# Gate and up products of a decoder layer's last two row groups: VectorE's order written out, both pairs in one chain of blocks, whole weight sums per transfer, input sums stored unsplit

## The chip, the cores and the metric

The kernel runs on one core of a Trainium2 chip. The metric is the device time of one execution in microseconds. Beside it stands one profiled execution, in which the start, the length and the waits of every instruction were recorded. The engines are TensorE (PE, its weight loads are PEld), VectorE (DVE), ScalarE (ACT), GpSimd (POOL) and SyncE (SP), whose instruction queue issues nearly all transfers of the part of the program that is changed.

## The reference

One layer of a hybrid decoder on 2048 rows of 1024 numbers in float32. The change is in the feed-forward part:

```python
h = h + _rmsnorm(y, g_post_mix[l])
f_in = _rmsnorm(h, g_pre_ffn[l])
gt = jnp.einsum("bsd,df->bsf", f_in, w_gate[l])
up = jnp.einsum("bsd,df->bsf", f_in, w_up[l])
f = jnp.einsum("bsf,fd->bsd", jax.nn.silu(gt) * up, w_down[l])
h = h + _rmsnorm(f, g_post_ffn[l])
```

`w_gate` and `w_up` are 1024 x 2816, `w_down` is 2816 x 1024.

## The kernel before, in words

**The arithmetic.** Every float32 operand of a product is split into a high part H (a copy to a narrower type, on ScalarE) and a low part L (the difference, on GpSimd or VectorE). A product is three products of halves, L x H, H x H and H x L. Here that is 4 slices of the inner dimension x 3 = 12 matmuls of 128x128 by 128x512.

**The fast multiplication.** The rows are taken in four groups of 512. Groups 0 and 1 form the first pair, groups 2 and 3 the second. For a pair, each block of the weights (two column tiles of 128, `i` = 0 for gate and 1 for up, `j` = 0 to 10) is a 2x2 matrix product, done by a Strassen-Winograd scheme with seven products (numbered 1 to 7) instead of eight. Weight sums S (numbers 3, 5, 6, 7) and `w_down` sums were computed and stored to DRAM during the attention part. Product 1 plus 2 (called `c11`) and, for the first pair, product 4 (`p4`) were computed there too and are only loaded.

**The stage that is changed** is the tail after attention. `five(g, B, todo)` (L1078) runs over 22 blocks of a pair: four products per block for the first pair (6, 5, 7, 3), five for the second (6, 5, 7, 4, 3). It is called twice, for g = 0 and then for g = 2, and each call begins with a first block of its own and ends by storing what is left.

**One block.** Two PSUM banks are used, `b2` and `b3`. Product 6 goes into `b2`, product 5 into `b3`. VectorE keeps `u2 = b2 + s1` (L1103; `s1` is one half of c11). Product 7 is added into `b2`; then VectorE reads `u3 = b2 + s1` (L1116), for the first pair adds `u3` to `p4` (L1119), and forms `u3 = b3 + u3` (L1120). Product 6 of the next block comes before product 4 (added into `b2`, so after L1116) and product 3 (added into `b3`, so after L1120). L1131 and L1134 read the final `b2` and `b3`. The four results of a gate block are put through a sigmoid on ScalarE (L1052) and multiplied on VectorE (L1053); those of an up block are multiplied into them (L1057). After each up block `hidden` forms the hidden sums with four VectorE additions, all between SBUF tiles (L1063 to L1066), and queues seven tiles for storing.

**Weights.** `weights` (L1019) loads a block's four sums S as four transfers into two `raw` tiles of 128x1024, copies each to `wH` (L1044, ScalarE) and subtracts to `wL` (L1045, GpSimd). There are three `wH` and three `wL` buffers and two are used per block, so a split can begin when an older product ends: the first of a block's two when product 3 of two blocks before ends, the second when product 5 of the block before ends.

**Beside the first pair** run the rest of the mixing part of group 3 (`residual`, L702, VectorE's L712 among it) and, for k = 0 to 3, `input_sums` (L860): it transposes rows of groups 2 and 3 on TensorE (L865), forms five input sums on VectorE and GpSimd (L887 to L897), splits each into H and L, and stores both. They are loaded again as operands of the second pair.

**What sets the order.** The tile framework orders each engine's queue by a simulated time of readiness. The matmuls of `product` are pinned by `keep_in_program_order`: each behind the instruction that stands before it on its engine as the code is written. VectorE, ScalarE, GpSimd and SyncE are ordered by the framework. `flush(2)` after each product puts up to two stores into SP's queue.

## Time and profile before

| | us |
|---|---|
| median of 3 runs | 2673.92 |
| lowest and highest run | 2673.45, 2678.8 |
| the profiled execution, its own time | 2673.32 |
| its span, first to last instruction | 2671.3 |
| first matmul of the first pair's blocks | starts at 1573.49 |
| first matmul of the down projection behind the second pair | starts at 2225.03 |

The changed part is the stretch between the last two rows. A line of the chain of waits has a start, a length, and what the work that ended last was doing in that time. A line of the timeline has start, length, engine, source line, operation, tiles and their count; in brackets stands how long the engine was idle before, and who ended that. A line of the waits names who waited for whom, the total, how often, and the longest. PEclk is the clock granted to TensorE, 1.00 being full speed. Names in front of an arrow are written, those behind it read; the order of the lines here is that of the program on the chip.

### The profile page before, as it was taken

Reading aid. Unit: us, or ns where it says so; the run is one execution under the profiler, and the core shown is the slowest. Engines: PE = TensorE matmul, PEld = TensorE weight load, DVE = VectorE, ACT = ScalarE, POOL = GpSimd, SP = SyncE. Lnnn points to the kernel's source line nnn. Section 1 sums busy time; section 2 is a strip of 40 time slices with the busy share of each in tenths; the row PEclk is TensorE's granted clock in tenths of the full one; section 3 lists DMA queues with packets and bytes.
Section 4 is the critical chain, followed back from the end, with each engine's and each line's share of the span. In section 5 each row is a group of like instructions: output and inputs, shape, how many; then the busy total and the mean of one; then the engine's idle time right before and its main releaser. Section 6 shows DMA issues by size and latency. Waiting matters only on the chain.

```text
span 2671.3 us, 35972 instructions
## 1 busy us (share of the span) xinstructions
PE 2470.6 (92%) x11156; PEld 1975.3 (74%) x11156; DVE 1880.6 (70%) x2405; ACT 1286.5 (48%) x2307; POOL 1449.7 (54%) x1760
## 2 busy tenths in 40 slices
PE   8989988997989999899999798889899999999998
PEld 6777766775767788587788576667677777887786
DVE  5787479978998756777775547877666775557556
ACT  4355546556655655666666543322222224444543
POOL 6655587467765656448434236653333234557556
PEclk9999999998989999999999898999999999999999
DMA  9999879986898888757876467896755558667654
GB/s 346 317 315 317 270 243 329 329 295 206 289 328 266 270 280 295 256 158 237 281 227 231 161 215 256 304 330 217 260 176 180 180 165 276 193 195 264 215 190 169
DMA packets 315103, 669.92 MB, mean 251 GB/s; under 512 B 36768, under 2 KB 44960, under 8 KB 314912
## 3 DMA queue, kind: packets, MB, share of 16 engines
q1 hardware_dynamic: 290624, 634.60, 71.4%
q10 hardware_dynamic: 24288, 33.04, 3.5%
q8 instruction: 88, 1.44, 0.2%
q14 instruction: 103, 0.84, 0.1%
HBM read 467.22 MB, written 200.28 MB: 250 GB/s over the span
## 4 chain that ended last, share of the span: by engine, by line
PE 60%; DVE 15%; DMA 11%; POOL 5%; issue 5%; ACT 2%; SPq 1%; POOLq 0%; ACTq 0%; DVEq 0%
PE dps L749 13%; PE b L749 12%; PE c L749 9%; PE inps L253 3%; PE inps L255 3%; PE inps L257 3%; PE at L585 3%; DVE om L568 2%; PE p L749 2%; PE o L591 2%; PE z L558 2%; DVE cv L473 2%; PE ops L686 1%; PE z L559 1%; PE o L590 1%
## 5 line engine op out<-in xcount | busy, mean ns | idle before, releaser
L569 POOL TENSOR_TENSOR A<-A,om 128x512 f32<-128x512 f32 (+2 forms) x320 | 312.9, 978 | 346.9 <-DVE om L568 311.8
L568 DVE TENSOR_TENSOR_SCAN om<-om,one,z 128x513 f32<-128x513 f32 (+2 forms) x320 | 351.3, 1112 | 110.4 <-ACT A L566 100.4
L1045 POOL TENSOR_TENSOR wL<-raw,wH 128x1024 fp32r<-128x1024 f32 x88 | 218.7, 2487 | 368.0 <-ACT wH L1044 343.0
L473 DVE SCALAR_TENSOR_TENSOR cv<-glu,cw,cv 128x512 f32<-128x512 f32 x464 | 346.4, 747 | 5.9
L1194 DVE TENSOR_TENSOR xL__22254<-t__22256,xH__22253 128x512 fp32r<-128x512 f32 x154 | 199.6, 1304 | 157.3 <-ACT xH__22253 L1193 157.1
L1192 POOL TENSOR_TENSOR xL__22252<-t__22255,xH__22251 128x512 fp32r<-128x512 f32 x154 | 208.2, 1357 | 175.0 <-ACT xH__22251 L1191 174.4
L253 PE MATMUL inps<-xH,wL 128*128 128x512 f32 x640 | 261.5, 409 | 1.8 <-DVE qkL L246 1.4
L255 PE MATMUL inps<-xH,wH 128*128 128x512 f32 x640 | 258.5, 405 | 0.0
L257 PE MATMUL inps<-xL,wH 128*128 128x512 f32 x640 | 258.1, 404 | 0.0
L246 DVE TENSOR_TENSOR TL<-at,TH 128x512 fp32r<-128x512 f32 (+1 forms) x320 | 189.3, 598 | 88.1 <-ACT TH L245 87.6
L749 PE MATMUL dps<-xH__22251,xL__22254 128*128 128x512 f32 x616 | 242.2, 393 | 7.3 <-DVE xL__22254 L1194 5.6
L564 ACT ACTIVATE om<-z 128x512 f32<-128x512 f32 (+2 forms) x320 | 171.3, 536 | 161.2 <-PE z L559 68.1
L749 PE MATMUL dps<-xL__22252,xH__22253 128*128 128x512 f32 x616 | 241.9, 393 | 3.0 <-POOL xL__22252 L1192 3.0
L749 PE MATMUL dps<-xH__22251,xH__22253 128*128 128x512 f32 x616 | 241.6, 392 | 0.0
L823 POOL TENSOR_TENSOR sum<-sum 128x512 f32<-128x512 f32 x132 | 172.8, 1309 | 116.1 <-DMA sum<-in_w_down_dram 37.2
L207 ACT ACTIVATE wH<-raw 128x1024 fp32r<-128x1024 f32 x156 | 165.7, 1062 | 104.3 <-DMA raw<-in_w_in_dram 36.6
L245 ACT ACTIVATE TH<-at 128x512 fp32r<-128x512 f32 (+1 forms) x320 | 167.9, 545 | 87.3 <-PE at L585 78.5
L1191 ACT ACTIVATE xH__22251<-t__22255 128x512 fp32r<-128x512 f32 x154 | 97.2, 631 | 233.3 <-POOL xL__22252 L1192 148.2
L585 PE MATMUL at<-idr,A 128*128 128x128 f32 x1088 | 191.5, 280 | 11.8 <-ACT ma L625 3.6
L566 ACT ACTIVATE A<-z 128x512 f32<-128x512 f32 (+2 forms) x320 | 167.8, 538 | 21.9 <-PE at L585 20.2
L585 PEld LDWEIGHTS at<-idr,A 128*128 128x128 f32 x1088 | 141.6, 144 | 49.2 <-POOL A L569 6.3
L1044 ACT ACTIVATE wH<-raw 128x1024 fp32r<-128x1024 f32 x88 | 93.1, 1058 | 147.9 <-PE b L749 120.1
(310 smaller groups left out, 6359.0 us busy)
## 6 DMA issues: line engine op xcount, KB each, us to landing
wL<-wL SPq DMA_DIRECT2D x156, 512.0 KB, 4.6
raw<-S SPq DMA_DIRECT2D x176, 256.0 KB, 4.1
raw<-in_w_in_dram SPq DMA_DIRECT2D x80, 512.0 KB, 6.1
t__22256<-u SPq DMA_DIRECT2D x154, 256.0 KB, 2.7
S<-sum SPq DMA_DIRECT2D x88, 256.0 KB, 4.8
c<-c ACTq DMA_DIRECT2D x88, 256.0 KB, 4.4
t__22255<-wd SPq DMA_DIRECT2D x88, 256.0 KB, 2.9
K<-kd SPq DMA_DIRECT2D x80, 256.0 KB, 4.4
```

Of the source, the lines that this page charges most:

```text
L246: nc.vector.tensor_tensor(L, ps, H.bitcast(F32), ALU.subtract)
L253: nc.tensor.matmul(ps, WL[:, kc], aH[t](k), start=k == 0, stop=False)
L255: nc.tensor.matmul(ps, WH[:, kc], aH[t](k), start=False, stop=False)
L257: nc.tensor.matmul(ps, WH[:, kc], aL[t](k), start=False, stop=k == KT - 1)
L473: nc.vector.scalar_tensor_tensor(to, gl[c][:, k:k + G], cw[:, c, k:k + 1], a, ALU.mult, ALU.add))
L568: nc.vector.tensor_tensor_scan(r, r, z[:, 0:1].to_broadcast([P, w + 1]), one, ALU.mult, ALU.bypass)
L569: nc.gpsimd.tensor_tensor(a[:, 0:w], a[:, 0:w], om[:, G - w + 1:G + 1], ALU.mult)
L585: nc.tensor.transpose(pt[:, j * P:(j + 1) * P], u["A"][j][:, b * P:(b + 1) * P], id32)
L749: return nc.tensor.matmul(ps, a, b, skip_group_check=True, **flags)
L1045: nc.gpsimd.tensor_tensor(L, r, f32(H), sub)
L1192: nc.gpsimd.tensor_tensor(WL, w, f32(WH), sub)
L1194: nc.vector.tensor_tensor(UL, t, f32(UH), sub)
```

## The change

1. **VectorE.** All additions and products of a block go through `dve`, which pins them in the order in which the code is written. The multiplication by the loaded c11 comes after L1120's addition and after product 6 of the next block. The last result of a block and the hidden sums (`behind`) stand after product 5 of the next block.
2. **One chain.** Both pairs are one list of 44 blocks and `five` runs once.
3. **Weights.** Two sums lie in one DRAM tile and come in one transfer. The split is done by halves of 512 columns: two ScalarE copies and two GpSimd subtractions per `raw` tile in place of one each.
4. **Hidden sums.** The three that are additions stay in one tile of three parts (`acc`), the same one for every j, and leave as one transfer `u3`. A result is put into SP's queue two products later than before at the earliest.
5. **Input sums.** `input_sums` stores numbers 3, 5, 6, 7 unsplit, in one DRAM tile each, and splits number 4 directly into the operand where it is used. The other four are split when they are loaded (`sum_in`), 7 with VectorE, the rest with GpSimd. `residual` and `input_sums` are cut into steps that the blocks call one by one.

The core of the diff:

```diff
-    def sum_in(g, n, H, L):
+    def sums_split(HL, k, t, eng=nc.gpsimd):
+        H, L = (m[:, k, :] for m in HL)
+        nc.scalar.activation(H, t, AF.Copy)
+        eng.tensor_tensor(L, t, f32(H), sub)
+
+    def sum_in(g, n, H, L, eng=nc.vector):
         for k in range(4):
             t = ev("sumin")
-            nc.sync.dma_start(t, stored["B", g, n, k])
-            nc.scalar.activation(H[:, k, :], t, AF.Copy)
-            nc.vector.tensor_tensor(L[:, k, :], t, f32(H[:, k, :]), sub)
+            nc.sync.dma_start(t, stored["B", g, n][:, k, :])
+            sums_split((H, L), k, t, eng)
...
         def halves(n, t):
-            if banks is not bank:
-                store(t, "B", g, n, k)
-                return
-            H, L = ev("bH", F32R), ev("bL", F32R)
-            nc.scalar.activation(H, t, AF.Copy)
-            nc.gpsimd.tensor_tensor(L, t, f32(H), sub)
-            store(f32(H), "B", g, n, k, 0)
-            store(f32(L), "B", g, n, k, 1)
+            if n == 4 and t4:
+                sums_split(t4, k, t)
+            else:
+                part(t, k, TT, "B", g, n)
...
-                for t, n in zip(two(r), ns):
-                    nc.sync.dma_start(t, stored["S", i, j, n])
+                nc.sync.dma_start(r, stored["S", i, j, ns].rearrange("p n t -> p (n t)"))
...
-                nc.scalar.activation(H, r, AF.Copy)
-                nc.gpsimd.tensor_tensor(L, r, f32(H), sub)
-                A[ns[0]], A[ns[1]] = zip(two(H), two(L))
+                for n, h, l, t in zip(ns, two(H), two(L), two(r)):
+                    nc.scalar.activation(h, t, AF.Copy)
+                    nc.gpsimd.tensor_tensor(l, t, f32(h), sub)
+                    A[n] = h, l
+                yield
...
+        def dve(*args):
+            tc.keep_in_program_order(nc.vector.tensor_tensor(*args))
...
-            s1, s2, s4 = (next(us) for _ in range(3))
+            s1, s2, s4 = us
...
+            late.append([1, sums3, "u3", g, j])
...
         def flush(n):
-            for _ in range(min(n, len(late))):
-                store(*late.pop(0))
+            for e in late:
+                e[0] -= 1
+            while n and late and late[0][0] < 0:
+                store(*late.pop(0)[1:])
+                n -= 1
...
                 b.mul(b3, 5, True)
                 nxt = Block(n + 1) if n + 1 < NB else None
+                for fn, *args in behind:
+                    fn(*args)
+                c11 = result(b.i, (1, 1), b.c11)
                 b.mul(b.b2, 7, False)
                 u3 = next(u_)
-                nc.vector.tensor_tensor(u3, b.b2, b.s1, add)
+                dve(u3, b.b2, b.s1, add)
                 p4_ = b.A.get("p4")
                 if p4_ is not None:
-                    nc.vector.tensor_tensor(p4_, u3, p4_, add)
-                nc.vector.tensor_tensor(u3, b3, u3, add)
+                    dve(p4_, u3, p4_, add)
+                dve(u3, b3, u3, add)
                 if nxt:
                     next(nxt.ahead)
                     nxt.first()
-                out((1, 1), b.c11)
+                for fn, *args in early.get(n, ()):
+                    fn(*args)
+                c11()
...
-        five(0, B, todo)
-        B2.update(operands(NG - 2, [(7, e[4:6]), (3, e[0:2]), (4, e[2:4])]))
-        five(NG - 2, B2, {})
+        todo[2 * HF - 1] = [(operands, last, [(3, e[0:2])], nc.gpsimd)]
+        five({2 * HF - 1: [(operands, last, [(7, e[4:6])])]}, todo)
```

How VectorE's queue stands now, at two places. The first place is in the second pair, where an up block ends and the next gate block is under way. Before, from the last read of `b3` (L1134) over the four hidden sums (L1063 to L1066) to the reads that products 4 and 3 wait for (L1116, L1120):

```order
L1134 TENSOR_TENSOR b3_20940<-b3_20940,cs_17578 128x512
L1057 TENSOR_TENSOR accf_17579<-b3_20940,accf_17579 128x512
L1063 TENSOR_TENSOR sumf_17582<-accf_17579 128x512
L1064 TENSOR_TENSOR sumf_17583<-sumf_17582,accf_17579 128x512
L1065 TENSOR_TENSOR accf_17579<-accf_17579 128x512
L1066 TENSOR_TENSOR lng_117<-accf_17579,sumf_17583 128x512
L1053 TENSOR_TENSOR accf_17579<-a22_21159,accf_17579 128x512
L1116 TENSOR_TENSOR cs_17578<-b2_20984,glu0_132 128x512
L1120 TENSOR_TENSOR cs_17578<-b3_21036,cs_17578 128x512
```

After, the same place of another up block (all of `dve` has the line L1068; `a22` holds the loaded c11):

```order
L1068 TENSOR_TENSOR b3_20364<-b3_20364,glu3_138 128x512
L1068 TENSOR_TENSOR rbf_17521<-b3_20364,rbf_17521 128x512
L1068 TENSOR_TENSOR accf_17520<-rbf_17521,lng_117 128x512
L1068 TENSOR_TENSOR accf_17520<-accf_17520,sumf_17524 128x512
L1068 TENSOR_TENSOR rbf_17521<-rbf_17521,sumf_17524 128x512
L1068 TENSOR_TENSOR accf_17520<-accf_17520 128x512
L1068 TENSOR_TENSOR glu3_138<-b2_20408,glu0_132 128x512
L1068 TENSOR_TENSOR glu3_138<-b3_20458,glu3_138 128x512
L1068 TENSOR_TENSOR sumf_17522<-a22_20377,sumf_17522 128x512
```

The product with c11 (L1053, `a22`) stood between the hidden sums and the read of `b2`; it now stands behind both reads.

The second place is in the first pair, where the input sums of k = 0 begin (their two VectorE products are L906 and L907 now, L887 and L888 before). After, from the last read of `b3` of an up block to the next block's read of `b3`:

```order
L1068 TENSOR_TENSOR b3_18131<-b3_18131,cy_17518 128x512
L1068 TENSOR_TENSOR lng_117<-b3_18131,lng_117 128x512
L1068 TENSOR_TENSOR accf_17520<-lng_117,sumf_17523 128x512
L1068 TENSOR_TENSOR accf_17520<-accf_17520,sumf_17522 128x512
L1068 TENSOR_TENSOR lng_117<-lng_117,sumf_17522 128x512
L906 SCALAR_TENSOR_TENSOR tmp_18248<-b12_18251,gpf_120,piece_18261 128x512
L1068 TENSOR_TENSOR accf_17520<-sumf_17524,accf_17520 128x512
L907 SCALAR_TENSOR_TENSOR lnb_118<-b12_18251,gpf_120,tmp_18248 128x512
L1068 TENSOR_TENSOR cy_17518<-b2_18186,glu0_132 128x512
L1068 TENSOR_TENSOR a22_18146<-cy_17518,a22_18146 128x512
L1068 TENSOR_TENSOR cy_17518<-b3_18222,cy_17518 128x512
```

Before, from the same read of `b3` on, at the first of the four such places:

```order
L1134 TENSOR_TENSOR b3_18004<-b3_18004,glu3_138 128x512
L1057 TENSOR_TENSOR accf_17579<-a22_18121,accf_17579 128x512
L1057 TENSOR_TENSOR accf_17579<-b3_18004,accf_17579 128x512
L1063 TENSOR_TENSOR sumf_17582<-accf_17579,sumf_17581 128x512
L1064 TENSOR_TENSOR sumf_17583<-sumf_17582,rbf_17580 128x512
L1065 TENSOR_TENSOR accf_17579<-accf_17579,rbf_17580 128x512
L1066 TENSOR_TENSOR lng_117<-accf_17579,sumf_17583 128x512
L1116 TENSOR_TENSOR glu3_138<-b2_18046,glu0_132 128x512
L887 SCALAR_TENSOR_TENSOR tmp_18280<-b12_18281,gpf_120,piece_18292 128x512
L1053 TENSOR_TENSOR accf_17579<-a22_18212,accf_17579 128x512
L1119 TENSOR_TENSOR a22_18017<-glu3_138,a22_18017 128x512
L888 SCALAR_TENSOR_TENSOR lnb_118<-b12_18281,gpf_120,tmp_18280 128x512
```

Between L1116 and L1119, and between L1119 and L1120 (which follows two rows later), other instructions stood; now the three reads of `b2`, `p4` and `b3` stand together, and both products of the input sums stand ahead of them. On TensorE the transposes of the next k (`b12`, whose PSUM bank L907 must have left) stand between product 7 and product 6 of the next block. After:

```order
L755 MATMUL b2_18186<-e5__17562,wH_18202 128x512
L886 MATMUL b12_18555<-idr_72,big_17244 128x128 x2
L886 MATMUL b12_18555<-idr_72,big_17245 128x128 x2
L755 MATMUL b2_18288<-xH__17525,wL_18283 128x512
L755 MATMUL b2_18288<-xH__17525,wH_18282 128x512
```

Before:

```order
L749 MATMUL b2_18154<-xL__17585,wH_18150 128x512
L865 MATMUL b12_18522<-idr_72,big_17303 128x128 x2
L865 MATMUL b12_18522<-idr_72,big_17304 128x128 x2
L865 MATMUL b22_18527<-idr_72,big_17303 128x128 x2
L865 MATMUL b22_18527<-idr_72,big_17304 128x128 x2
L749 MATMUL b3_18104<-e0__17638,wL_18063 128x512
```

Before, these transposes stood one product later, between product 6 of the next block (`xL`) and product 3 (`e0`), and both banks of a k together; now the first bank's are in front of product 6 and the second bank's behind it.

More of the change, by code (lines that the diff above doesn't have):

```diff
@@ L702, in residual, with residual_parts @@
     def residual(T, keep=False):
+        for _ in residual_parts(T, keep):
+            pass
+    def residual_parts(T, keep):
         g, t = divmod(T, TT)
@@ L1107, in five @@
                 pass
+            b.split()
             b.first()
+            b.second()
+            behind = []
             for n in range(NB):
-                out = times_up if b.i else gated
                 b3 = gu("b3")
@@ L1136, in five @@
                 if b.i:
[L1137 removed]
+                    behind.append((hidden, b.g, b.j))
+                behind += todo.get(n, ())
                 b = nxt
[L1139 to L1151 removed]
@@ L1153, in layer_kernel, with steps @@
-        for t in range(TT):
-            todo[t] = [(residual, (NG - 1) * TT + t, True)]
-            todo[2 * t + TT + 1] = [(tprep2, t)]
-        R = []
-        B2 = {}
-        def second():
+            for fn, *args in behind:
+                fn(*args)
+            assert next(more, None) is None
+            for _ in range(9):
+                flush(2)
+        operands(0, [(6, x2), (5, x2), (7, e[4:6]), (3, e[0:2])])
+        R = []
+        last = NG - 2
+        def steps():
+            parts = [residual_parts((NG - 1) * TT + t, True) for t in range(TT)]
+            for t in range(TT + 1):
+                for p in parts[max(t - 1, 0):t + 1][::-1]:
+                    next(p)
+                yield
+            t = rp.tile([P, D], F32, tag="gain", name="tmp", bufs=1)
+            tmp = [*two(t), free[12], free[2]]
+            B[last][4] = operand(*e[2:4])
+            for k in range(TT):
+                yield from input_sums(last, k, tmp, bank, B[last][4])
@@ L1171, in layer_kernel @@
+        more = steps()
+        todo = {n: [(next, more)] * (1 if n < 5 else 2 - n % 2) for n in range(16)}
+        todo[17] = todo[18] = [(next, more)]
+        todo[2 * HF - 1] = [(operands, last, [(3, e[0:2])], nc.gpsimd)]
+        five({2 * HF - 1: [(operands, last, [(7, e[4:6])])]}, todo)
         r = [(R[0], f"t{i}") for i in range(4)]
```

160 lines of the change are left out of this document (84 added, 76 removed).

## The prediction

> **What bounds the kernel now.** First the page: which engine is busy, and how much.
>
> ```profile
> span 2671.3 us, 35972 instructions
> PE 2470.6 (92%) x11156; PEld 1975.3 (74%) x11156; DVE 1880.6 (70%) x2405; ACT 1286.5 (48%) x2307; POOL 1449.7 (54%) x1760
> ```
>
> TensorE bounds the kernel as a whole, so a gain must be a gap or a slow stretch of TensorE that goes. The change touches only the stretch from 1573.4 to 2225.0 us. The windows view of the pinned matmuls gives it in two parts, first pair and second pair (span of the window, PE busy with the count, PEld, clock, DMA share, GB/s). Two 20 us windows inside the second pair, over all instructions, show the pace with and without a wait:
>
> ```profile
> 1573.40:1888.40 315.00, 268.26 (x1057) 208.24 (x1058) 0.93 0.79 270
> 1888.40:2225.00 336.60, 317.24 (x1321) 251.71 (x1320) 0.98 0.59 196
> 1980.00:2000.00 20.00, 18.19 (x72) 14.25 (x71) 14.09 (x16) 5.25 (x7) 4.81 (x2) 0.91 0.51 164
> 2000.00:2020.00 20.00, 20.00 (x87) 16.07 (x87) 13.18 (x16) 5.48 (x6) 8.70 (x4) 1.00 0.46 148
> ```
>
> At full pace a matmul takes 20.00/87 = 0.23 us, a product of 12 takes 2.76 us. So the first pair's 1057 matmuls need 243 us of 315, the second's 1321 need 304 of 336.6: 72 and 33 us are lost, some 5 of them to 32 transposes. The waits of TensorE in this stretch tell to whom (total, times, longest):
>
> ```profile
> PE b L749 <- DVE cs L1120: 11.5, 4, 3.3
> PE b L749 <- DVE cy L1120: 10.7, 5, 3.7
> PE b L749 <- DVE glu L1120: 7.9, 4, 5.2
> PE b L749 <- POOL wL L1045: 6.8, 5, 3.2
> PE b L749 <- DVE glu L1116: 6.6, 4, 1.8
> PE b L749 <- DVE cy L1116: 6.1, 4, 2.1
> PE b L749 <- DVE cs L1116: 5.5, 3, 1.8
> PE b L865 <- ACT tmp L886: 3.3, 1, 3.3
> PE b L865 <- DVE lnb L888: 1.8, 1, 1.8
> PE b L749 <- DVE glu L1103: 1.7, 1, 1.7
> ```
>
> These sum to 61.9 us. L1120 (30.1 us) holds product 3 in the first pair, L1116 (18.2 us in 11 waits) product 4 in the second. The rest of the loss is clock: 0.07 x 315 = 22 us and 0.02 x 336.6 = 7 us, 29 together, part of it inside the waits.
>
> The chain of waits shows one such place whole, the end of an up block in the second pair:
>
> ```profile
> 1982.87 0.71 DVE b L1134
> 1983.60 0.70 DVE accf L1057
> 1984.33 2.69 DVE sumf L1063
> 1987.04 2.77 DVE sumf L1064
> 1990.34 0.69 DVE lng L1066
> 1991.05 0.64 ACT accf L1052
> 1991.71 0.69 DVE accf L1053
> 1992.41 0.61 DVE glu L1116
> 1993.06 21.42 PE b L749 x84
> 2014.51 0.71 DVE b L1134
> 2044.59 0.71 DVE b L1134
> ```
>
> GpSimd's timeline at the same place, and TensorE's first matmul after the wait:
>
> ```profile
> 1984.06 2.40 POOL L1045 TENSOR_TENSOR wL<-raw,wH 128x1024 fp32r<-128x1024 f32 x1 [8.34 <-ACT wH L1044]
> 1986.87 2.40 POOL L1045 TENSOR_TENSOR wL<-raw,wH 128x1024 fp32r<-128x1024 f32 x1 [0.40 <-ACT wH L1044]
> 1993.06 0.86 PE L749 MATMUL b<-e__19975,a22h 128*128 128x512 f32 x2 [1.81 <-DVE glu L1116]
> ```
>
> The reader is to see three things. The first two hidden sums take 2.69 and 2.77 us in place of 0.7, because each ends 0.55 us after a GpSimd subtraction ends (1984.06 + 2.40 = 1986.46, L1063 ends at 1987.02). Behind the sums VectorE waits for the sigmoid of c11 and multiplies by it, 1.4 us, before it reads `b2`. TensorE was free at 1993.06 - 1.81 = 1991.25. And the two rounds of a pair of blocks differ, 31.64 us (1982.87 to 2014.51) and 30.08 us.
>
> **The change part by part.**
>
> *Second pair, written order.* c11's product moves behind the reads, so 1.4 us goes from this path; nobody waits for it there. It could hold the queue later, where it waits for c11's transfer, but next wanted of VectorE are L1120's read, now ahead of it, and the last read of `b2` a product of 2.76 us later. The GpSimd work is now four subtractions of 512 columns. Their price is in the first pair, with VectorE in the way or not:
>
> ```profile
> 1644.44 1.72 POOL L879 TENSOR_TENSOR bL<-tmp,bH 128x512 fp32r<-128x512 f32 x1
> 1647.80 1.28 POOL L879 TENSOR_TENSOR bL<-tmp,bH 128x512 fp32r<-128x512 f32 x1
> 1645.61 1.10 DVE L1057 TENSOR_TENSOR accf<-a,accf 128x512 f32<-128x512 f32 x1
> ```
>
> 1.28 us alone, 1.72 when a VectorE operation between SBUF tiles slips in between two. I step through the place at 1982.87. The copy of half a tile on ScalarE takes 0.64 (the row of L1052), so the first piece runs from 1983.6 to 1984.9 and the first sum ends 0.55 later, at 1985.5. The second piece then goes until 1986.7 and the second sum ends at 1987.3; the third piece until 1988.5 and sum 1989.1; the fourth until 1990.3 and sum 1990.8. The read of `b2` has a PSUM operand, which no row shows held up, and ends at 1991.5. TensorE wants it at 1991.25: 0.3 us of wait with the signal's 0.05, in place of 1.81. The bounds are nothing (the pieces come between other work) and 0.8 (GpSimd does its pieces without a gap, 2 x 2.6 us, and the sums follow). Ten places at 0.3 and the last one, where the down projection's splits stand in VectorE's queue, unchanged at 1.1: 18.2 becomes 4.1, **14 us saved**.
>
> *First pair, written order.* The same steps hold, but product 3 needs two more operations, `p4` and `b3`, at 0.7 each: the read ends at 1991.5 + 1.4 in that count, a wait of 1.7 us. That is for six of the ten up blocks. At the second, residual's product stands ahead of the sums; at the third and the fourth one, L906 and L907 (the products of the input sums) do:
>
> ```profile
> 1620.05 1.28 DVE L712 SCALAR_TENSOR_TENSOR big<-big,rs,gain 128x1024 f32<-128x1024 f32 x1
> 1642.02 0.73 DVE L887 SCALAR_TENSOR_TENSOR tmp<-b,gpf,piece 128x512 f32<-128x512 f32 x1
> ```
>
> So 1.7 + 1.3 = 3.0 at the second. At the third and fourth the transposes of the next k stand in TensorE's queue ahead of product 6, and wait for the bank that L907 leaves: the four sums end 7.9 us after the block's end, with both products 9.4, and TensorE comes there after two products, 5.6 us: 3.8 us each, and within it the reads for product 3 get done. At the fifth, the last two additions of the input sums stand between: 1.7 + 1.4 = 3.1. Sum 10.2 + 3.0 + 7.6 + 3.1 = 24. To this the start (1.7, unchanged), 0.6 left of the waits for `wL`, and 2.0 at the junction of the pairs: there three of the four VectorE splits of operand 7 at 0.7 each stand ahead of the read of `b3`. That makes 28.3 for the first pair's 43.7 (all rows but L1116's). **15 us saved.** Bounds: the extra operations may fall into VectorE's pauses, then 10 waits at 1.0 remain (13 with the start and the junction, 30 saved); or the four GpSimd pieces do not fit between and the wait stays what it is (0 saved).
>
> *Clock.* The 31.64 us round has the slow window, 72 matmuls after a 1.81 us wait; the other one hasn't. A slow stretch costs a good 1.5 us. In the second pair ten waits of 0.3 should bring none: 7 becomes 1. In the first I take it as going with the waits: 22 x 28.3/43.7 = 14. **14 us saved**; between 0 (the gate answers to something else) and 23.
>
> The row says that waits of 1.8 us suffice now and then. The Trainium skill, page "TensorE: Matmul & The Clock Gate", section "HAM oscillation — how this bites in real kernels", has it that gaps have to exceed about 3.4 us before the clock is halved. By that rule the second pair's slow stretches would not come from these waits and stay, and the sum would come out 6 us higher.
>
> *Fewer transfers.* The rows of transfers in this stretch (count, KB, us to landing):
>
> ```profile
> raw<-S SPq DMA_DIRECT2D x170, 256.0 KB, 4.1
> u<-lng SPq DMA_DIRECT2D x21, 256.0 KB, 3.5
> B<-bH SPq DMA_DIRECT2D x20, 256.0 KB, 3.9
> B<-bL SPq DMA_DIRECT2D x20, 256.0 KB, 5.0
> ```
>
> The input sums' 40 stores and 40 loads become 16 and 16; the 170 loads of weights half as many of double size. TensorE waits for none of these directly; they act through `wL`, whose 6.8 us I took off above except 0.6. What is moved to the load side is GpSimd work: seven operations per k become three, and twelve come back when operands 6, 5 and 3 are split. GpSimd has room (its 4.8 us per block in blocks of 11 and 14 us). Priced at nothing; if that cover goes, operand 3's four splits (4 x 1.28 among the weights' pieces) could come 2 us late, once.
>
> *Chain.* The second call's first block ran alone only in the code; TensorE shows no wait for its loads. Nothing.
>
> Sum against the profiled execution's own 2673.32 (its span 2671.3 and 2.0 around it; the median of the runs is 2673.92, 0.6 more): 14 + 15 + 14 = 43, so 2630. The median should shift alike: **2630 us**.
>
> **The rivals.**
>
> *Nearly all waits go* (VectorE's extra operations find pauses everywhere). For it: VectorE is busy 13.18 of 20 us in the undisturbed window. Against: the count above has no pause before the read in an up block. Waits 61.9 to 15, clock 29 to 6: 70 saved, 2603.
>
> *Only the moved product counts*: GpSimd's four pieces hold VectorE for as long as the two did. For it: the total of GpSimd's work is the same. Against: the sum of steps above uses the slower alternation and still fits. Second pair 18.2 to 6.5, first pair 43.7 to 38, clock 29 to 24: 22 saved, 2651.
>
> *The clock does not follow the waits.* Its loss stays, 2644. The rule quoted above is a weaker form; the 72 against 87 matmuls speak against it.
>
> *Slower: one set of sum tiles.* The next up block's first sum must wait until `u3` has left, where before three tiles rotated among others. `u3` is three times the 256 KB that take 3.5 us to land, 10.5 us at most. It enters SP's queue two products after the sums are written at the earliest, some 14 us after the block's end, and lands at 24.5; the next first sum is due 29 us after the block's end. That leaves 4.5 us. But SP's queue is held up in order:
>
> ```profile
> SPq L755 <- DVE sumf L1063: 44.4, 10, 5.1
> ```
>
> If it is late by more than these 4.5, VectorE stops at the sum, with the read of `b2` and so products 4 and 3 behind it, at each of 20 up blocks. At 4 us past the slack that is 80 lost against 43 won: 2673.3 + 37 = 2710. It decides from 2.2 us past the slack on. Against: in the row the holds are what the stores themselves wait for, and these now come later than the sums.
>
> *It does nothing that shows* (within 0.2%, some 5 us, about what a measurement of this kernel can tell): the waits go and others of the same length come, for the sigmoids or c11, now that VectorE cannot pass one by. 2673.
>
> **How the numbers follow.** Chances: the forecast 0.58, nearly all waits gone 0.13, only the moved product 0.11, clock unmoved 0.08, slower 0.06, nothing 0.04. Faster by over 0.2% is the sum of the first four, 0.90; same 0.04; slower 0.06. The forecast's own range is its bounds: 14 to 17, 0 to 30, and 0 to 23 of the three terms, not all at one end, say 2610 to 2648. With the two nearest cases on both sides the range is 2600 to 2654.
>
> **What would show it.** In the profile after: L1068's reads end at most 0.8 us behind TensorE in the second pair, its rounds are all near 28 us, and PEclk is 1.00 there; the hidden sums take 1.2 to 1.8 us each and never 2.7; TensorE's waits in the first pair are about 1.7 us at up blocks, with two of 3.8 for the transposes. I am wrong if the second pair's rounds stay over 29 us, if TensorE waits for a first hidden sum that waits for a transfer of `u3`, or if the down projection, which is not touched, takes other than its 446 us.

## The result and the profile after

The changed kernel takes 2629.89 us (median of four runs, 2626.07 to 2632.92), the kernel before beside it 2675.99: a ratio of 0.983 with a 95% interval of 0.981 to 0.985. That is faster, as forecast, and 0.1 us from the forecast time. So close a hit is luck: the four runs lie 7 us apart, and the same kernel measured once more had a median of 2634.55. Its profiled execution took 2632.4 us. First its page:

```profile
span 2630.6 us, 35776 instructions
PE 2460.1 (94%) x11156; PEld 1970.1 (75%) x11156; DVE 1859.7 (71%) x2409; ACT 1290.7 (49%) x2395; POOL 1482.0 (56%) x1844
```

GpSimd has 32 us more to do, with 84 more instructions, and VectorE 21 us less. The windows of the pinned matmuls, first and second pair:

```profile
1579.40:1872.40 293.00, 260.26 (x1068) 203.44 (x1068) 0.97 0.75 258
1872.40:2185.50 313.10, 309.88 (x1311) 246.18 (x1310) 0.99 0.59 200
```

Each pair is shorter by 22 to 24 us (315.00 and 336.60 before). From the first pinned matmul to the first of the down projection, "the touched stretch" from here on, it is 605.9 us in place of 651.5: 45.6 saved. The profiled executions differ by only 40.9 us, since the stretch began 6.1 us later (1579.6 against 1573.5); the down projection takes 445.2 in place of 446.2. TensorE's waits in the stretch:

```profile
PE b L755 <- POOL wL L1061: 14.0, 7, 6.0
PE b L755 <- DVE glu L1068: 6.9, 5, 2.3
PE b L755 <- DVE cs L1068: 6.0, 3, 3.0
PE b L755 <- DVE cy L1068: 4.5, 4, 1.6
```

With two of 1.0 and 0.5 us for the transposes they sum to 32.9 us (61.9 before in the rows of the prediction; two smaller waits of 0.7 and 0.3 us make it 62.9). VectorE's share fell from 51.8 in those rows to 17.9, and `wL`, GpSimd's half of the weights' split, rose from 6.8 to 14.0. VectorE's queue at the end of an up block of the second pair, and the first sum of the next one:

```profile
2015.71 0.69 DVE L1068 TENSOR_TENSOR sumf<-b,sumf 128x512 f32<-128x512 f32 x1
2016.44 1.15 DVE L1068 TENSOR_TENSOR accf<-sumf,rbf 128x512 f32<-128x512 f32 x1
2017.62 1.67 DVE L1068 TENSOR_TENSOR accf<-accf 128x512 f32<-128x512 f32 x1
2019.21 1.78 DVE L1068 TENSOR_TENSOR sumf<-sumf,accf 128x512 f32<-128x512 f32 x1
2020.92 1.77 DVE L1068 TENSOR_TENSOR accf<-sumf,accf 128x512 f32<-128x512 f32 x1
2022.62 0.68 DVE L1068 TENSOR_TENSOR cs<-b,glu 128x512 f32<-128x512 f32 x1
...
2044.65 1.15 DVE L1068 TENSOR_TENSOR accf<-rbf,lng 128x512 f32<-128x512 f32 x1
```

The four sums take 1.15 to 1.78 us each, and the read of `b2` for product 4 follows them at once. A round is 2044.65 - 2016.44 = 28.21 us (31.64 and 30.08 before). TensorE no longer stops here: in the chain of waits one piece without a break runs from the end of the first pair to the splits of the down projection:

```profile
1879.80 284.79 PE b L755 x1211
```

The new cost lies in the first pair. The timelines of ScalarE, GpSimd and TensorE around the longest wait:

```profile
1726.73 0.63 ACT L802 ACTIVATE e__18249<-piece 128x512 fp32r<-128x512 f32 x1 [12.13 <-DVE piece L918]
1727.27 1.13 ACT L1060 ACTIVATE wH<-raw 128x512 fp32r<-128x512 f32 x2
...
1729.11 2.95 POOL L1061 TENSOR_TENSOR wL<-raw,wH 128x512 fp32r<-128x512 f32 x2
...
1730.89 0.79 PE L755 MATMUL b<-xH__17525,wL 128*128 128x512 f32 x1 [6.00 <-POOL wL L1061]
```

In ScalarE's queue the copy for the direct split of input sum number 4 (L802) waits 12.13 us for VectorE's last addition (L918), which stands behind the four hidden sums of the up block in VectorE's queue. The weights' copies (L1060) stand behind that copy, so `wL` comes late and TensorE has nothing to multiply for 6.00 us.

### The profile page after: what moved, and what is told of

It reads as the page before. It is cut to its first block, busy times and chain, and to the rows that moved or that the text cites. A ratio compares the mean times of both kernels' runs of the same rounds, so it can differ in the third digit from the quotient of the medians.

```text
span 2630.6 us, 35776 instructions
## 1 busy us (share of the span) xinstructions
PE 2460.1 (94%) x11156; PEld 1970.1 (75%) x11156; DVE 1859.7 (71%) x2409; ACT 1290.7 (49%) x2395; POOL 1482.0 (56%) x1844
## 4 chain that ended last, share of the span: by engine, by line
PE 61%; DVE 15%; DMA 10%; POOL 6%; issue 5%; ACT 2%; SPq 1%; POOLq 0%; DVEq 0%; ACTq 0%
PE b L755 16%; PE dps L755 13%; PE c L755 9%; DVE om L568 3%; PE at L585 3%; DVE cv L473 2%; PE inps L253 2%; PE inps L255 2%; PE inps L257 2%; PE p L755 2%; PE o L591 2%; PE z L558 2%; PE ops L686 1%; PE ops L684 1%; PE ops L685 1%
## 5 line engine op out<-in xcount | busy, mean ns | idle before, releaser
L1061 POOL TENSOR_TENSOR wL<-raw,wH 128x512 fp32r<-128x512 f32 x176 | 257.2, 1489 | 283.7 <-ACT wH L1060 283.7
L207 ACT ACTIVATE wH<-raw 128x1024 fp32r<-128x1024 f32 x156 | 165.6, 1062 | 104.1 <-DMA raw<-in_w_in_dram 42.7
L245 ACT ACTIVATE TH<-at 128x512 fp32r<-128x512 f32 (+1 forms) x320 | 167.7, 543 | 90.8 <-PE at L585 82.5
L558 PE MATMUL z<-K,QL 128*128 128x512 f32 (+2 forms) x320 | 132.4, 415 | 29.4 <-DVE om L568 24.0
```

The lines of the kernel that those rows point to most:

```text
L1061: nc.gpsimd.tensor_tensor(l, t, f32(h), sub)
```

## The experiments

Times of different kernels are compared as ratios to the kernel before on the same chip. The touched stretch of the profile is finer: three profiles in which it runs the same work in the same order gave 605.9, 605.5 and 604.6 us. The waits of the table include the few that the profile puts down to no other engine (0.7 us in before, 1.6 in order_alone, 0.5 in s_paired).

| kernel | touched stretch, us | TensorE's waits in it, us | median, us | ratio to before, 95% interval |
|---|---|---|---|---|
| before | 651.5 | 62.9 | 2675.99 | 1 |
| changed | 605.9 | 32.9 | 2629.89 | 0.981 to 0.985 |
| again | 605.5 | 32.2 | 2634.55 | 0.981 to 0.986 |
| order_off | 634.0 | 52.3 | 2663.39 | 0.991 to 0.996 |
| wide | 618.9 | 40.8 | 2650.10 | 0.986 to 0.992 |
| split4_later | 599.0 | 28.1 | 2626.69 | 0.978 to 0.983 |
| order_alone | 665.5 | 82.5 | 2690.44 | 1.004 to 1.007 |
| s_paired | 649.8 | 62.8 | 2680.83 | 0.999 to 1.002 |
| s_single | 599.4 | 29.3 | 2629.52 | 0.979 to 0.985 |
| u3_later | 604.6 | 32.2 | 2631.07 | 0.982 to 0.986 |
| one_go | 604.4 | 32.7 | 2634.11 | 0.981 to 0.984 |
| old_input | 606.6 | 35.5 | 2632.82 | 0.981 to 0.984 |
| one_go_old_input | 632.8 | 58.7 | 2660.21 | 0.991 to 0.995 |
| both | 599.3 | 29.4 | 2626.13 | 0.979 to 0.983 |

**The changed kernel once more** (again).

> The changed kernel unaltered, once more, beside the variants. It shows how far two profiles of it differ. The touched stretch (first pinned matmul to the first matmul of the down projection) should take 606 us again, within 2. The stretch began 6.1 us later in the profile after (1579.57) than in the one before (1573.49). If that was the clock of one execution, it begins some us elsewhere now; if it is the paired stores of the weights' sums, it begins at 1579 to 1580 again. TensorE's waits for wL should be 14 us again, the longest 6.0, if they come from the order of ScalarE's queue.

The stretch took 605.5 us, and the waits for `wL` were 14.0 with a longest of 6.0 again, so these belong to the order of the queues. The stretch began at 1584.0, 4.4 us later than in the first profile of the same kernel.

**VectorE not pinned** (order_off):

```diff
-            tc.keep_in_program_order(nc.vector.tensor_tensor(*args))
+            nc.vector.tensor_tensor(*args)
```

> The changed kernel without the pinning of VectorE: everything else stays, the scheduler sets VectorE's order, and it puts c11's product (0.7 us, and up to 0.7 of waiting for the sigmoid) ahead of the reads of b2 and b3 again, in an up block the next block's split of a22 too. Theory: 1.4 us come back at ten places of the second pair and nine of the first, 27 us, and with them some 10 us of clock, so 2660 to 2670, and second-pair waits of 1 to 2 us at the up blocks. Rival (the halves on GpSimd and the fewer transfers did it, not the order): within 8 us of the changed kernel, 2630 to 2638.

The stretch grew by 28 us, and the time lies in the expected interval. An up block's end in the second pair, on VectorE and then on TensorE:

```profile
1987.14 1.78 DVE L1068 TENSOR_TENSOR accf<-accf 128x512 f32<-128x512 f32 x1
1989.61 0.69 DVE L1068 TENSOR_TENSOR accf<-a,accf 128x512 f32<-128x512 f32 x1 [0.70 <-ACT accf L1075]
1990.22 1.41 DVE L1068 TENSOR_TENSOR glu<-b,glu 128x512 f32<-128x512 f32 x2
...
1990.96 0.72 PE L755 MATMUL b<-e__18249,a22h 128*128 128x512 f32 x2 [1.39 <-DVE glu L1068]
```

Behind the last sum VectorE waits 0.70 for the sigmoid and multiplies for 0.69, and only then reads `b2`. These 1.4 us come back as a wait of 1.39 us on TensorE, almost without loss: in the changed kernel the read comes just in time, with nothing in hand. Eight other up blocks show the same, 1.36 to 1.39 us each. The rival, by which the halves and transfers alone did it, falls: without the order the rest of the change takes 17.5 us off the stretch (651.5 to 634.0), with it 45.6. TensorE's waits for VectorE are 49.3 us here (17.9 with the order), those for `wL` 3.0 (14.0 with it). So most of the new waits for `wL` come, or come to light, with the order; which of the two was not taken apart.

**Whole tiles again** (wide):

```diff
-                for n, h, l, t in zip(ns, two(H), two(L), two(r)):
-                    nc.scalar.activation(h, t, AF.Copy)
-                    nc.gpsimd.tensor_tensor(l, t, f32(h), sub)
-                    A[n] = h, l
+                nc.scalar.activation(H, r, AF.Copy)
+                nc.gpsimd.tensor_tensor(L, r, f32(H), sub)
+                A[ns[0]], A[ns[1]] = zip(two(H), two(L))
```

> The changed kernel with the weights split by whole tiles again, one copy and one subtraction of 1024 columns in place of two of 512. Theory: the first two hidden sums take 2.7 us again in place of 1.2 to 1.8, the path to the read of b2 grows by about 2 us, of which the second pair has 1.5 in hand: waits of some 0.5 at ten places, and in the first pair 1 to 2 us more at nine, with a little clock 2640 to 2650. Rival (GpSimd's pieces hold VectorE for as long as the two wide ones): the sums' total time and the time stay, 2628 to 2633.

```profile
1974.83 2.68 DVE L1067 TENSOR_TENSOR accf<-rbf,lng 128x512 f32<-128x512 f32 x1
1977.54 2.77 DVE L1067 TENSOR_TENSOR accf<-accf,sumf 128x512 f32<-128x512 f32 x1
1980.23 0.68 DVE L1067 TENSOR_TENSOR rbf<-rbf,sumf 128x512 f32<-128x512 f32 x1
1980.84 0.68 DVE L1067 TENSOR_TENSOR accf<-accf 128x512 f32<-128x512 f32 x1
1981.44 1.40 DVE L1067 TENSOR_TENSOR glu<-b,glu 128x512 f32<-128x512 f32 x2
...
1982.17 0.73 PE L755 MATMUL b<-e__18221,a22h 128*128 128x512 f32 x2 [0.42 <-DVE glu L1067]
```

As expected the sums take 2.68 and 2.77 us again, and TensorE waits 0.42 us at each of ten places. But the path itself is only 0.4 us longer: 6.61 us from the first sum to the read, against 6.18 in the changed kernel, whose four sums are all slowed a little where here two are slowed much. I had put it at 2 us. The rival's premise, that the sums take about as long in all, holds; its conclusion, that the time stays, does not, since there is no slack to take up even 0.4 us. The stretch is 13.0 us longer, and the median stands at the upper end of the expected interval. About 6 of the 13 us lie in the second pair, 4.3 of them in these ten waits, and about 7 in the first, where up blocks wait 1.9 us in place of 1.5 and the waits behind the input sums moved.

**Number 4 split when it is loaded** (split4_later):

```diff
-                yield from input_sums(last, k, tmp, bank, B[last][4])
+                yield from input_sums(last, k, tmp, bank)
...
+        todo[16] = [(operands, last, [(4, e[2:4])], nc.gpsimd)]
```

> The changed kernel with input sum number 4 stored unsplit like the other four and split when it is loaded, behind block 16, in place of being split as it is made. Theory: the copy for the direct split stands in ScalarE's queue and waits there for VectorE (16.8 us in three waits, the longest 12.1), with the weights' copies behind it; without it TensorE's waits for wL fall from 14.0 us to about 4, with the clock 9 to 12 us less: 2618 to 2621. Rival (GpSimd has simply too much to do there): four subtractions are only moved from blocks 6 to 13 to block 16, the waits for wL move to 1800 us and sum to 10 or more, 2627 to 2633.

```profile
PE b L755 <- POOL wL L1061: 9.7, 6, 3.0
```

The stretch is 6.9 us shorter and the wait of 6.00 is gone, so the direct split did stand in the way. But the theory had `wL` fall to 4 us, and 9.7 are left: the scheduler placed the loaded splits among the weights' copies soon after their data came, and a wait of 2.2 us stands behind one of them now (and behind a sigmoid that waits 3.17 us for VectorE). The median lies next to the rival's interval and 6 us above the theory's. Half right, the rest by the rival.

**The order alone, in the kernel before** (order_alone): all VectorE operations of a block through `dve`, in the changed kernel's order, the rest of the kernel as before.

> The kernel before with VectorE's order alone: all of a block's VectorE operations pinned in the changed kernel's order (c11's product behind the reads, the last result and the hidden sums behind product 5), the weights' splits whole tiles of 1024, transfers, input sums and the two chains as before. Theory (order and half tiles add up): in the second pair the waits of 1.81 become about 0.4, as in the run with wide splits, its rounds 28.6 us, and the stretch of 651.5 us becomes 615 to 625, 2637 to 2650 in all. Rival (the order needs the other parts, since pinned operations stand behind the input sums' own): the second pair gains its 15 us and the first pair nothing, a stretch of 632 or more, 2655 or more.

The theory falls. The rival has the direction and the reason, pinned operations behind those of the input sums, but was far too mild: the kernel became 0.5% slower than before. In the second pair the theory holds for product 4, whose waits are 0.44 us (1.81 before), though TensorE now waits 0.5 to 2 us for `wL` in each round, so the pair is only some 4 us shorter in place of 15. The first pair lost far more than the rival's nothing. One of its two waits of 15 us, with VectorE's and SP's queues ahead of it, in order of time:

```profile
1680.98 1.75 DVE L1051 TENSOR_TENSOR lng<-rbf,sumf 128x512 f32<-128x512 f32 x1
...
1682.75 0.32 SPq L755 DMA_DIRECT2D u<-lng  x1
1683.16 0.88 SPq L1032 DMA_DIRECT2D raw<-S  x2
1684.14 0.38 SPq L755 DMA_DIRECT2D B<-bL  x1
1684.57 0.42 SPq L870 DMA_DIRECT2D piece<-fx  x1
...
1688.91 0.69 DVE L896 TENSOR_TENSOR piece<-piece,glu 128x512 f32<-128x512 f32 x1 [6.18 <-DMA piece<-fx]
1691.46 0.69 DVE L897 TENSOR_TENSOR piece<-piece 128x512 f32<-128x512 f32 x1 [1.86 <-DMA piece<-fx]
1692.07 0.68 DVE L1051 TENSOR_TENSOR cy<-b,glu 128x512 f32<-128x512 f32 x1
...
1694.26 0.80 PE L749 MATMUL b<-e__17638,wL 128*128 128x512 f32 x1 [15.12 <-DVE cy L1051]
```

Two queues hold each other up, each by its order. The load of a piece stands in SP's queue behind the store of a hidden sum (`u<-lng`), which waits until VectorE has written it. VectorE's addition of that input sum (L896) then waits 6.18 us for the piece, and behind it, in the written order, the reads that TensorE waits for.

**What the written order needs** (one_go, old_input, one_go_old_input). Of the change's other parts two could keep the pieces' loads clear: that the input sums are cut into steps, so that a piece is asked for a step ahead of its use, and that they are stored unsplit, 16 stores in place of 40. Each was undone alone, then both. In one_go:

```diff
-                yield from input_sums(last, k, tmp, bank, B[last][4])
+                for _ in input_sums(last, k, tmp, bank, B[last][4]):
+                    pass
+                yield
...
-        todo = {n: [(next, more)] * (1 if n < 5 else 2 - n % 2) for n in range(16)}
+        todo = {n: [(next, more)] for n in (0, 1, 2, 3, 4, 5, 7, 9, 11)}
```

> The changed kernel with the four k of the input sums called as one step each, at blocks 5, 7, 9 and 11 as in the kernel before, in place of four steps each over the blocks 5 to 15. It asks why the written order alone, put into the kernel before, was 0.5% slower: there VectorE's two additions of an input sum (waiting 6 to 8 us for pieces whose loads stood in SP's queue behind stores) held up the pinned reads behind them, and TensorE waited 15 us at two up blocks. Theory A (the cut into steps cures it, since the loads are asked for a step ahead): here the waits of 10 to 15 us are back at two to four up blocks, the first pair is 20 to 40 us longer, the stretch 626 to 645 us, 2650 to 2670. Theory B (the unsplit stores cure it, 16 in place of 40 in SP's queue): the stretch is 604 to 612 us, 2628 to 2637.

In old_input, besides number 4 as in split4_later and plain loads of the halves in `operands`:

```diff
-            if n == 4 and t4:
-                sums_split(t4, k, t)
-            else:
-                part(t, k, TT, "B", g, n)
+            H, L = ev("bH", F32R), ev("bL", F32R)
+            nc.scalar.activation(H, t, AF.Copy)
+            nc.gpsimd.tensor_tensor(L, t, f32(H), sub)
+            store(f32(H), "B", g, n, k, 0)
+            store(f32(L), "B", g, n, k, 1)
```

> The changed kernel with the input sums stored in two split halves and loaded without a split, number 4 too, as in the kernel before, and still called in steps: 40 stores and 40 loads in place of 16 and 16. Theory A (the cut into steps is the cure): no wait of over 5 us comes back, number 4's copy no longer waits in ScalarE's queue, GpSimd has 12 subtractions fewer later and 13 more among the steps: a stretch of 598 to 610 us, 2623 to 2635. Theory B (fewer stores are the cure): waits of 10 us or more for VectorE at two or more up blocks, a stretch of 622 us or more, 2647 or more.

> The changed kernel with both undone that singly cost nothing: the input sums called as one step each (alone 604.4 us of stretch) and stored in split halves (alone 606.6). Theory A (either of the two is enough to keep the loads of the pieces clear of the stores, so the loss of the order alone in the first pair needs both): two or more waits of 10 us or more for VectorE in the first pair, a stretch of 622 to 645 us, 2645 to 2670. Theory B (neither has to do with it; the rest of the change, half tiles, the copy of a22 asked for a step behind its load, or one chain, is what the written order needs): a stretch of 602 to 612 us, 2627 to 2638.

Alone, neither costs anything in sum: 604.4 and 606.6 us of stretch, the changed kernel's 605.9. That is theory B in the first run and A in the second, which contradict each other as single causes. It is a balance in both: TensorE waits longer for VectorE (21.5 and 29.8 us in place of 17.9) and less for `wL` (7.8 and 4.6 in place of 14.0). And old_input has one wait of 9.9 us, where theory A allowed none of over 5: VectorE waits 12.07 us there for a piece. Both undone cost 27 us, the stretch and time of theory A, though only one of its two waits of 10 us or more came (16.26 us; the next ones are 8.82 and 5.91). VectorE behind the hidden sums of an up block of the first pair, and TensorE, at the longest:

```profile
1740.91 1.77 DVE L1077 TENSOR_TENSOR accf<-accf 128x512 f32<-128x512 f32 x1
1749.89 0.69 DVE L921 TENSOR_TENSOR piece<-piece,glu 128x512 f32<-128x512 f32 x1 [7.22 <-DMA piece<-fx]
1755.28 0.69 DVE L922 TENSOR_TENSOR piece<-piece 128x512 f32<-128x512 f32 x1 [4.70 <-DMA piece<-fx]
1755.89 0.68 DVE L1077 TENSOR_TENSOR glu<-b,glu 128x512 f32<-128x512 f32 x1
...
1758.08 0.80 PE L755 MATMUL b<-e__17579,wL 128*128 128x512 f32 x1 [16.26 <-DVE glu L1077]
```

It is the picture of order_alone: in SP's queue the load of the first piece, issued at 1743.55, stands behind the stores of two hidden sums. So the written order needs one of the two to escape most of the loss (the steps alone leave old_input's wait), and the change has both. The whole tiles' 13 us and these 27, if they add up, which no run tried, make 40 of the 60 us by which order_alone's stretch is longer than the changed kernel's; the other 20, and what the single chain of 44 blocks gives, were not taken apart.

**Paired weights' sums** (s_paired in the kernel before, s_single in the changed one): one load of 512 KB or two of 256 KB. The core of s_single, which s_paired reverses:

```diff
-                nc.sync.dma_start(r, stored["S", i, j, ns].rearrange("p n t -> p (n t)"))
+                for t, n in zip(two(r), ns):
+                    nc.sync.dma_start(t, stored["S", i, j, n])
```

> The kernel before with the weights' sums in paired DRAM tiles alone: the sums numbered 6 and 5, and 7 and 3, lie side by side, stored by two transfers as before and loaded by one. It asks why the touched stretch begins at 1579.6 to 1584.0 us in the five profiles of kernels with the paired tiles and at 1573.5 in the one without. Theory (the stores into rows of twice the length take longer and hold up the stretch ahead): it begins at 1579 to 1584 here too, and the time is 5 to 10 us above the kernel before. Rival (it differs from one execution to the next): it begins at 1576 or below, or the time is within 4 us of the kernel before. In the stretch itself half as many loads of weights change TensorE's waits for wL (6.8 us) by less than 2 us.

> The changed kernel with the weights' sums in DRAM tiles of their own again, loaded by two transfers of 256 KB in place of one of 512 KB. Theory of the paired stores: the stretch begins at 1573 to 1577 us, and the time is 5 to 8 us less, 2622 to 2626. Rival: it begins at 1579 to 1584 as before, and the time is that of the changed kernel within 4 us. In both the stretch itself takes 606 us within 3, since TensorE waits for none of these loads.

The stretch began at 1583.4 us in s_paired and at 1587.1 in s_single. In all the profiles it begins between 1573.5 and 1587.1, with paired tiles between 1577.9 and 1584.0, and neither time differs from that of its base. So the times give the theory of slow paired stores no support, and two profiles of one kernel, the changed one, already begin 4.4 us apart. A cost of a few us at the start is not excluded: three of the four profiles without paired tiles begin ahead of all ten with them (1573.5 to 1577.5), the fourth, s_single, behind them all. The second half of both expectations failed as well. TensorE's waits for `wL` came to 4.0 us with the loads paired in the kernel before (6.8 there), and to 9.8 with them single in the changed one (14.0 there), whose stretch is 6.5 us shorter: no rule that one form is better, but not nothing either.

**The hidden sums' store later** (u3_later):

```diff
-            late.append([1, sums3, "u3", g, j])
+            late.append([5, sums3, "u3", g, j])
```

> The changed kernel with the store of the three hidden sums put into SP's queue four products, 11 us, later. By the slower rival of the prediction (one set of sum tiles, 4.5 us of slack) that is 6.5 us past the slack, VectorE stops at the first hidden sum at each of 20 up blocks with product 4 behind it, and 80 to 130 us are lost: 2710 or more. By the profile of the changed kernel (the three sums leave as soon as the last one is written, 1937.97 us, land 4.2 us later, and the next first sum comes at 1959.9, a slack of 18 us) nothing happens: 2627 to 2636, a stretch of 606 us within 2.

The edit did not do what it says. SP's queue has the store right behind the last sum all the same (the row of VectorE, then SP's):

```profile
2017.82 1.78 DVE L1068 TENSOR_TENSOR accf<-sumf,accf 128x512 f32<-128x512 f32 x1
...
2019.63 0.32 SPq L761 DMA_DIRECT2D u<-accf  x1
```

The scheduler places the transfer where it can go, whatever the code's count says. The run tells nothing of the slack; that is read from the changed kernel's own profile, where the 22 stores of 768 KB land 4.1 us after their issue (median) and the next first sum comes 22 us after the last one's end: 18 us in hand. A store that comes too late was not tried.

**Both improvements together** (both): split4_later and s_single.

> The changed kernel with number 4 split when it is loaded and the weights' sums in DRAM tiles of their own, the two edits that shortened the touched stretch from 605.5 to 599.0 and 599.4 us. Theory (they remove different waits, the 6.00 us behind number 4's split in one, the 2.97 and 2.98 us at the residual and the third k in the other): the waits for wL fall to 5 to 7 us, the stretch to 593 to 597, 2617 to 2624. Rival (both only shift ScalarE's queue against TensorE at the same few places): 598 to 602 us, 2622 to 2629.

The waits for `wL` fell to 6.0 us, as the theory has it, and the stretch stayed at 599.3, as the rival has it: the waits for VectorE grew from 17.9 to 21.7 us. By its stretch each of the three variants (split4_later, s_single, both) is better than the changed kernel by 6.5 to 7 us; by their times only the ratios' middles are lower (0.981 to 0.982 against 0.983), and the intervals overlap. All of them beat the kernel before.

## Why the prediction was right, point by point

*Second pair, written order: 14 us.* Right. Waits of 0.3 us at ten places were forecast, and there are none; the end waits 2.33 us, not 1.1. So 18.2 became 2.3, 15.9 saved. The count of steps (sums end at 1990.8, TensorE wants `b2` at 1991.25) was good to 0.3 us: order_off adds 1.4 to the path and gets 1.39 of wait.

*Half tiles.* The expected 1.2 to 1.8 us per sum are there. In the prediction's count they shorten the path by 0.2 us (the sums end at 1990.8, where L1066's row ends at 1991.03); wide measures 0.4.

*First pair, written order: 15 us, 28.3 of waits left.* 30.6 are left, so 13 saved, but that this came so near is luck: two errors cancel. The ten up blocks, put at 24 us, cost 12.9. Of the six put at 1.7 us, five waited 1.45 to 1.61 and the seventh not at all. The second, put at 3.0, waited 1.40; the third and the fourth, put at 3.8 each for the transposes, 0.44 and 3.50 (0.52 at the transposes, 2.98 at product 3). At the fifth, put at 3.1, no wait for VectorE is left, since TensorE has just waited 6.00 us for `wL`. The start cost 1.43 for 1.7; the junction's 2.0 became 0.97 for VectorE and 0.89 for `wL`. So this term was 11 us too high, and the next one 13 too low.

*`wL`: 0.6 left, "Priced at nothing".* This step failed: 14.0 us. The text looked at GpSimd's room, which is there, and not at what the moved splits wait for on ScalarE. Number 4's copy waits for VectorE ahead of the weights' copies; that is the wait of 6.00 us, and without it 9.7 of the 14 are left and the stretch is 6.9 us shorter (split4_later). Of these 9.7, 4.6 us are the two waits while residual's work goes on (1.60 and 2.97 in the changed kernel). What the rest comes from stays open.

*Fewer transfers and input sums: nothing.* Right for each alone, in sum, and wrong for both: without the steps and without the unsplit stores the changed kernel loses 27 us. The prediction took the written order for something that works by itself. order_alone, 0.5% slower than before, shows that it doesn't.

*Clock: 14 us.* By the windows 0.03 x 293 and 0.01 x 313, 12 us, are left of 29: 17 saved. It followed the waits, as forecast. Together 15.9 + 13.1 + 17 = 46, for 45.6 measured. The windows give the clock to two digits, which leaves each of the clock's terms open by 1.5 us, and part of it lies inside the waits, so this fit says less than it seems to.

*The slower rival.* Its slack of 4.5 us came from a store that enters SP's queue two products later. It enters at once, and the slack is 18 us; the mechanism was far from deciding. The other rivals are out by the rows: not nearly all waits went (32.9 left, for 15), and the clock did follow. That only the moved product counts was nearer than it looked. Its premise holds, that GpSimd's pieces hold VectorE for about as long as the two wide ones, and wide, with whole tiles, comes out near its figures (6.4 us of waits for VectorE in the second pair for 6.5, 2650 us for 2651, the latter with other waits in it). But TensorE had no slack behind the sums, so the 0.4 us that the halves do save count at each up block.

## What to carry to other kernels

To fix one engine's order by hand is to bind every operation in it to the latest input of the ones ahead of it: move loads a step ahead or stores away from that queue first, or the gain is a loss. An operation that moves to an engine with room still takes a place in its queue, so ask what it waits for, and who stands behind it, before it is priced at nothing. When two parts of a change each cost nothing to undo, undo both before calling them useless.

## What the runs showed of the hardware

TensorE's clock answers to waits of under 2 us. The windows of the pinned matmuls over 300 us of the second pair tell it. In the kernel before, with nine waits of 1.81 to 2.06 us:

```profile
1915.00:2215.00 300.00, 282.96 (x1177) 224.87 (x1176) 0.98 0.55 180
```

In order_off, with nine waits of 1.36 to 1.39 us:

```profile
1905.00:2205.00 300.00, 287.60 (x1224) 229.10 (x1223) 1.00 0.56 187
```

In the changed kernel, with none:

```profile
1875.00:2175.00 300.00, 299.11 (x1272) 237.88 (x1271) 1.00 0.58 197
```

Waits of 1.81 us go with a clock of 0.98, those of 1.38 us with 1.00. The loss comes right behind the wait, and not behind each: in the kernel before four of the nine waits are followed by 3.2 to 4.4 us of matmuls at half pace, 0.43 us apart in place of 0.23 (in s_paired, with nine waits of 1.81 to 1.83 us, three of nine), in order_off none. The 3.60 us behind one wait, in the kernel before and in order_off:

```profile
1993.10:1996.70 3.60, 3.60 (x9) 2.79 (x10) 0.56 0.93 285
1991.00:1994.60 3.60, 3.60 (x16) 2.93 (x17) 1.00 0.94 300
```

So the edge lies between 1.4 and 1.8 us, for waits some 30 us apart in an otherwise busy stretch; in the changed kernel's first pair waits of 1.60 and 1.61 us cost no clock either. Below it a wait costs its own length and no more: order_off's waits come 29.61 us apart (1961.35, 1990.96, 2020.57), 1.40 more than the changed kernel's round of 28.21. Above it the loss does not grow with the wait. In the changed kernel's first pair the waits of 2.97, 2.98 and 6.00 us are followed by 6.3, 3.6 and 3.4 us at half pace:

```profile
1656.50:1662.80 6.30, 6.29 (x15) 4.93 (x16) 0.51 0.99 324
1703.40:1707.00 3.60, 3.60 (x9) 2.82 (x10) 0.53 1.03 408
1730.90:1734.20 3.30, 3.30 (x8) 2.62 (x9) 0.50 1.04 349
```

Ahead of the first of these TensorE had already waited 1.04 us, with only two transposes between: 0.44 us of work in 4.45 us.

The Trainium skill, page "TensorE: Matmul & The Clock Gate", section "HAM oscillation — how this bites in real kernels", speaks of gaps of more than about 3.4 us. By that rule no wait of 1.81 us would have cost clock, and the second pair would have kept its loss; the measurement decides, and it has half pace behind such waits.

A VectorE operation between SBUF tiles is slowed by GpSimd's subtraction in pieces or as a whole for about as long in sum (6.18 us for four sums with halves, 6.61 with whole tiles, where 0.7 each is their time alone). What the halves change is who is held up: every sum a little, or two of them much.
